# A decoder trunk on one core: some steps take two pieces of background modulation, its totals are fp32 products of the running sum, and attention's first left sides are made in the stage of v

## The chip, the cores and the metric

The kernel runs on one core of one Trainium2 chip. The metric is the device time of one execution in microseconds (us), as the median of several runs. The engines are named as the profile names them: PE (TensorE matmuls), PEld (its weight loads), DVE (VectorE), ACT (ScalarE), POOL (GpSimd) and SP (SyncE, which issues most DMAs). Every engine works through its own instructions in a fixed order and waits where an instruction's input or buffer isn't ready.

## The reference

Two layers over x of 1024 positions by 1024 features. Layer 0 mixes tokens with a gated MLP over chunks, layer 1 with attention in three dilations; a dense squared-ReLU MLP follows each. Each of the four sub-layers is modulated by a vector c:

```python
def ada_mod(c, w, b):
    m = jax.nn.silu(c) @ w + b                 # w: 1024 x 3072
    shift, scale, gate = jnp.split(m, 3, axis=-1)
    return shift[:, None, :], scale[:, None, :], 1.0 + gate[:, None, :]

for i in range(DEPTH):                          # DEPTH = 2
    shift, scale, gate = ada_mod(c, ada_w[i, 0], ada_b[i, 0])
    h = x * (1.0 + scale) + shift
    y = mixer_a(h, ...) if i % 2 == 0 else mixer_b(h, ...)
    x = layer_norm(ALPHA * x + gate * y, ln_g[i, 0], ln_b[i, 0])
    shift, scale, gate = ada_mod(c, ada_w[i, 1], ada_b[i, 1])
    h = x * (1.0 + scale) + shift
    y = jnp.square(jax.nn.relu(h @ mlp_w_up[i])) @ mlp_w_down[i]
    x = layer_norm(ALPHA * x + gate * y, ln_g[i, 1], ln_b[i, 1])
```

In `mixer_b`, h @ w_qkv gives q, k and v for three dilations and 16 heads. All of it is fp32.

## The kernel before

One program, built by a framework that orders each engine's instructions, runs the sub-layers 0 to 3 one after the other: `mixer_a`, `mlp(1)`, `attention`, `mlp(3)`. An fp32 matrix product is three matmuls of fp32r parts: a source is split into a high part (a cast on ACT, L102) and a low part (source minus high part, on DVE, L103), and the three products that matter are summed in PSUM. Large products are done in a form with seven products of half-size blocks (named 1 to 7) instead of eight, so the "left" and "right" sides of a product are blocks or sums and differences of blocks. 12 matmuls of 128x512 make one product of the up stage.

**An MLP has two stages.** In the up stage 16 chunks (`ch`) each run seven products (PE L914); their lefts, made by `make_left` five products ahead, take one ACT cast and one DVE subtraction each. DVE also adds PSUM to what was kept (`part`, L932) and forms sums of hidden rows (`s`). In the down stage (PE L1072, tiles `psd`) the hidden rows are read back as `lraw`.

**The modulation of the coming sub-layers is made in the background.** `ada_steps` turns one half (512 columns) of shift (part 0), scale (part 1) or gate (part 2) into a group of 11 small functions: eight steps that load 128x512 of `ada_w` (tile `adaw`, two buffers) and add it, times silu(c), to the running sum `adaacc` (one DVE instruction, L125 or L128), then `bias_row`, `reduce` and `total`. `reduce` splits the running sum (`adahi` on ACT, `adalo` on DVE). `total` sums over the 128 partitions on PE: for shift and scale eight matmuls of two columns (L159, L160, tile `psa`), for gate two of 512. `tick(n)` runs the next n functions of the queue; `drain()` runs all that are left. In this text a group is called by its name in the tiles, sub-layer, part and half: `3_1_0` is the first half of scale of sub-layer 3.

- `mixer_a` queues 8 groups (88 functions), calls `tick(2)` 16 times and `tick(7)` eight times, then drains.
- `mlp(1)` queues 10 groups (110 functions: six of sub-layer 2, the four of shift and scale of sub-layer 3), calls `tick()` after each of the 98 products of chunks 2 to 15, then drains: 12 functions are left for the drain.
- `mlp(3)` queues the two gate groups of sub-layer 3.

**Attention** begins with `values_stage`, which computes v for all heads (PE L1266, tiles `psv`; its weights go through the row buffers `raw` of `wts` and `res` of `work`), and evicts v by ACT and DVE copies, from where POOL stores it. Then `project()`, a generator, makes q and k of one pair of heads and one dilation after the other, again with seven products (PE L1422, tiles `psqk`). Before its first product it loads four quarters of weights (`wq`, `wk`, 128x512, in a pool that is opened after the stage of v) and makes three lefts (products 1, 2, 6). Four products are run first, then the masks are made (`near` on POOL, `far` on DVE), then the rest.

Of the kernel before, what the change touches and what calls it, by code (L numbers as in the profile page):

```python
# [10 lines left out]
F32 = mybir.dt.float32  # L11
# [24 lines left out]
def trunk(ctx: ExitStack, tc: tile.TileContext, x, c, ada_w, ada_b, ln_g, ln_b, a_w_in, a_b_in,  # L36
# [73 lines left out]
    def ada_steps(j, order):  # L110
# [4 lines left out]
        for part, h in order:  # L115
# [21 lines left out]
            def reduce(part=part, h=h, box=box):  # L137
                nm = f"{j}_{part}_{h}"
                acc = box["acc"]
                hi, lo = (ada_p.tile([P, HALF], F32R, name=f"ada{m}_{nm}", tag=f"ada{m}") for m in ("hi", "lo"))  # L140
                if part == 2:
                    V.tensor_tensor(acc[0:1, :], acc[0:1, :], box["row"][0:1, :], op=ALU.add)
                split(hi[:], lo[:], acc[:])
                box["sum"] = (hi, lo)

            def total(part=part, h=h, box=box, w0=w0):
                nm = f"{j}_{part}_{h}"
                hi, lo = box["sum"]
                pst = bank("tr", f"psa_{nm}")
                if part == 2:  # L150
                    T.matmul(pst[:], ones_r[:], hi[:], start=True, stop=False)
# [5 lines left out]
                for k in range(4):  # L157
                    w = slice(k * P, (k + 1) * P)
                    T.matmul(pst[:, 2 * k : 2 * k + 2], hi[:, w], ones_r[:, 0:2], start=True, stop=False)  # L159
                    T.matmul(pst[:, 2 * k : 2 * k + 2], lo[:, w], ones_r[:, 0:2], start=False, stop=True)  # L160
                src = pst[:, 0:8].rearrange("p (k t) -> p k t", t=2)[:, :, 0]
# [14 lines left out]
            todo.append([lambda k=k, step=step: step(k) for k in range(KD)] + [bias_row, reduce, total])  # L176
# [597 lines left out]
    def mlp(j, before):  # L774
# [21 lines left out]
        with ExitStack() as ph:  # L796


            with ExitStack() as up:
# [182 lines left out]
                for n, (ch, p) in enumerate(seq):  # L982
# [7 lines left out]
                    if ch > 1:  # L990
                        tick()
# [193 lines left out]
    def attention(before):  # L1185
# [16 lines left out]
        with ExitStack() as ph:  # L1202
            homes = {p: pool(ph, f"form{p}", 1, side="right") for p in (4, 6, 5)}

            def values_stage():
                with ExitStack() as vs:
# [83 lines left out]
                    for n, s in enumerate(steps):  # L1290
# [12 lines left out]
                        if n + SPLITS < len(steps):  # L1303
                            prepare(*steps[n + SPLITS])

# [5 lines left out]
            def perm(t, g, half=None):  # L1311

                d = DILATION[g]
                if g == 0:
                    return t if half is None else t[:, half * HALF : (half + 1) * HALF]
                if g == 1:
                    v = t.rearrange("p (r i) -> p r i", r=d)
                    n = v.shape[2] // 2
                else:
                    v = t.rearrange("p (a b i) -> p a b i", b=2, i=S // d)  # L1320
                    n = v.shape[3] // 2
                return v[..., half * n : (half + 1) * n]

            def by_pos(t, g):

                if g == 0:
                    return t
                if g == 1:
                    return t.rearrange("p (i r) -> p r i", r=4)
                return t.rearrange("p (i b a) -> p a b i", b=2, a=8)  # L1330

            order = [(hp, g) for hp in range(N_PAIRS) for g in PATTERNS]
            got = [dict() for _ in order]
            pinned = []

            def quarter(name):
                return qp.tile([P, 4, P], F32, name=name, tag="wq", bufs=4)

            PRODUCTS = (1, 2, 6, 5, 7, 3, 4)
            after = {}  # L1340

            def project():

                seq = [(n, p) for n in range(len(order)) for p in PRODUCTS]
                raw, total, left, sums, kept = {}, {}, {}, {}, {}

                def load(n, X, kh):
                    if n >= len(order):
                        return
                    hp, g = order[n]  # L1350
                    c0 = g * 3 * D + X * D + hp * P
                    t = raw[n, X, kh] = quarter(f"w{'qk'[X]}{kh}_{hp}_{g}")
                    nc.sync.dma_start(t[:], b_w_qkv[0, kh * HALF : (kh + 1) * HALF, c0 : c0 + P].rearrange("(k p) n -> p k n", p=P))

                def make_left(n, p):
                    hp, g = order[n]
                    nm = f"{hp}_{g}_{p}"
                    l11, l12, l21, l22 = (raw.get((n, X, kh)) for X in range(2) for kh in range(2))

                    def total_tile():  # L1360
                        return qp.tile([P, 4, P], F32, name=f"ws_{nm}", tag="ws", bufs=2)

                    src = {1: l11, 2: l12, 4: l22}.get(p)
                    if p == 6:
                        t5, src = total[n, 5], total[n, 6] = total_tile(), total_tile()
                        V.tensor_tensor(t5[:], l21[:], l22[:], op=ALU.add)
                        sub(src[:], t5[:], l11[:])
                    elif p == 5:
                        src = total.pop((n, 5))
                    elif p == 7:  # L1370
                        src = total_tile()
                        sub(src[:], l22[:], total[n, 6][:])
                        sub(total[n, 6][:], l12[:], total[n, 6][:])
                    elif p == 3:
                        src = total.pop((n, 6))
                    t = left[n, p] = wts.tile([P, 2, 4, P], F32R, name=f"left_{nm}", tag="whi")
                    split(t[:, 0], t[:, 1], src[:])
                    for X, kh in {6: ((0, 0),), 5: ((0, 1),), 7: ((1, 0),), 4: ((1, 1),)}.get(p, ()):
                        load(n + 1, X, kh)
                    if p == 3:  # L1380
                        for key in ((n, X, kh) for X in range(2) for kh in range(2)):
                            del raw[key]

                AHEAD = 3
                for X in range(2):
                    for kh in range(2):
                        load(0, X, kh)
                lefts = [(n, p) for n in range(len(order)) for p in (1, 2, 6, 5, 7, 4, 3)]
                for s in lefts[:AHEAD]:
                    make_left(*s)  # L1390

                def evict(n, p, acc):
                    hp, g = order[n]

                    def out(nm, half):
                        return perm(got[n][nm][:], g, half)

                    if p in (1, 6, 5):
                        t = kept[p] = work.tile([P, HALF], F32, name=f"part{p}_{hp}_{g}", tag="h")
                        A.copy(t[:], acc[:])  # L1400
                        return
                    if p == 2:
                        for nm in "qk":
                            got[n][nm] = wts.tile([P, S], F32, name=f"{nm}_{hp}_{g}", tag="wlo")
                    if p == 4:
                        A.copy(out("k", 1), by_pos(acc[:], g))
                        return
# [4 lines left out]
                for i, (n, p) in enumerate(seq):  # L1412
                    if i + AHEAD < len(seq):
                        make_left(*lefts[i + AHEAD])
# [517 lines left out]
```

## Time and profile before

| | us |
|---|---|
| median of 3 runs | 2657.34 (2653.39 to 2660.51) |
| the profiled execution's own time | 2653.4 |
| its span | 2651.7 |
| PE busy | 2588.0 (98%) |
| DVE busy | 1898.6 (72%) |
| ACT busy | 1259.1 (47%) |
| mean granted clock of PE | 0.992 |

The profiled execution stands at the fast end of the three runs, 3.9 us (0.15%) under their median. A row of the timeline gives start, duration, engine, line, operation, output<-inputs, shape and count; in brackets stands how long the engine had been idle before and what ended that. A row of the windows gives, for a stretch of the span, the busy time of each engine, then PE's granted clock, the share of the DMA engines and GB/s. Matmul durations overlap: back to back at full clock a 128x512 matmul shows 0.39 and starts 0.227 after the last.

### The profile page before, as it was taken

Reading aid. Unit: us, or ns where it says so; the run is one execution under the profiler, and the core shown is the slowest. Engines: PE = TensorE matmul, PEld = TensorE weight load, DVE = VectorE, ACT = ScalarE, POOL = GpSimd, SP = SyncE. Lnnn points to the kernel's source line nnn. Section 1 sums busy time; section 2 is a strip of 40 time slices with the busy share of each in tenths; the row PEclk is TensorE's granted clock in tenths of the full one; section 3 lists DMA queues with packets and bytes.
Section 4 is the critical chain, followed back from the end, with each engine's and each line's share of the span. In section 5 each row is a group of like instructions: output and inputs, shape, how many; then the busy total and the mean of one; then the engine's idle time right before and its main releaser. Section 6 shows DMA issues by size and latency. Waiting matters only on the chain. (4 is left out here: it accounts for less than half of the span.)

```text
span 2651.7 us, 36843 instructions
## 1 busy us (share of the span) xinstructions
PE 2588.0 (98%) x13322; PEld 2080.0 (78%) x13322; DVE 1898.6 (72%) x3462; ACT 1259.1 (47%) x2431; POOL 185.6 (7%) x213
## 2 busy tenths in 40 slices
PE   7999999999999998999999999999999999999998
PEld 6788878888788887887777777777776888878887
DVE  4677798787789677443677777767659865677987
ACT  2343285555434444322555555556517555544432
POOL 0001100000000000011212221112100000000000
PEclk8999999999999999999999999999999999999999
DMA  7354437666865643542444454544862754495562
GB/s 247 115 183 130 134 112 227 216 228 227 297 218 189 227 151 112 159 159 96 115 132 125 128 158 112 155 131 128 286 202 104 226 194 146 157 330 170 180 209 80
DMA packets 329787, 457.05 MB, mean 172 GB/s; under 512 B 51532, under 2 KB 179956, under 8 KB 329604
## 3 DMA queue, kind: packets, MB, share of 16 engines
q1 hardware_dynamic: 316548, 408.55, 48.6%
q0 software_dynamic: 13056, 46.14, 5.0%
q8 instruction: 104, 1.70, 0.3%
q14 instruction: 79, 0.65, 0.1%
HBM read 346.00 MB, written 108.61 MB: 171 GB/s over the span
## 5 line engine op out<-in xcount | busy, mean ns | idle before, releaser
L1422 PE MATMUL psqk<-right,left 128*128 128x512 f32 x2016 | 523.5, 405 | 3.4 <-DVE left L103 2.2
L1422 PEld LDWEIGHTS psqk<-right,left 128*128 128x128 f32 x2016 | 363.4, 189 | 96.2 <-issue 15.3
L914 PE MATMUL psua<-right,left 128*128 128x512 f32 x1536 | 364.5, 390 | 3.5 <-ACT right L102 1.7
L1072 PE MATMUL psd<-rhi,lhi 128*128 128x512 f32 x896 | 350.2, 391 | 2.1 <-ACT part L945 2.1
L1072 PE MATMUL psd<-rlo,lhi 128*128 128x512 f32 x896 | 349.5, 390 | 0.9 <-DVE rlo L103 0.7
L1072 PE MATMUL psd<-rhi,llo 128*128 128x512 f32 x896 | 349.4, 390 | 0.0
L914 PEld LDWEIGHTS psua<-right,left 128*128 128x128 f32 x1536 | 286.9, 188 | 66.0 <-ACT right L102 2.6
L103 DVE TENSOR_TENSOR left<-ws,left 128x512 fp32r<-128x512 f32 x224 | 164.9, 737 | 144.9 <-ACT left L102 143.2
L1489 ACT ACTIVATE p<-p,stat 128x256 f32<-128x256 f32 (+2 forms) x384 | 161.7, 422 | 154.9 <-DVE stat L1487 154.1
L1266 PE MATMUL psv<-vwhi,right 128*128 128x512 f32 x672 | 211.7, 396 | 7.2 <-ACT right L102 7.2
L1072 PEld LDWEIGHTS psd<-rhi,lhi 128*128 128x128 f32 x896 | 168.6, 188 | 37.8 <-ACT part L945 3.0
L1072 PEld LDWEIGHTS psd<-rlo,lhi 128*128 128x128 f32 x896 | 168.6, 188 | 36.3 <-DVE rlo L103 1.6
L1072 PEld LDWEIGHTS psd<-rhi,llo 128*128 128x128 f32 x896 | 168.5, 188 | 35.1
L914 PE MATMUL psuc<-right,left 128*128 128x512 f32 x768 | 188.2, 391 | 0.5 <-ACT right L102 0.4
L102 ACT CAST left<-ws 128x512 fp32r<-128x512 f32 x224 | 138.5, 619 | 95.1 <-DVE ws L835 74.8
L914 PEld LDWEIGHTS psuc<-right,left 128*128 128x128 f32 x768 | 143.4, 188 | 30.9 <-DVE right L103 0.9
L1266 PEld LDWEIGHTS psv<-vwhi,right 128*128 128x128 f32 x672 | 127.1, 190 | 35.7 <-ACT right L102 7.6
L128 DVE SCALAR_TENSOR_TENSOR adaacc<-adaw,silu_c,adaacc 128x512 f32<-128x512 f32 x140 | 107.1, 765 | 65.4 <-DMA adaw<-in_ada_w_dram 64.7
L103 DVE TENSOR_TENSOR llo<-lraw,lhi 128x1024 fp32r<-128x1024 f32 x112 | 136.3, 1217 | 0.6 <-ACT lhi L102 0.6
L1266 PE MATMUL psv<-vwlo,right 128*128 128x512 f32 x336 | 132.7, 396 | 0.2 <-DVE r L215 0.2
L1487 DVE CUSTOM_DVE_ANT_0 p<-sc,bias 128x256 f32<-128x256 f32 (+2 forms) x384 | 103.1, 323 | 40.3 <-PE sc L1575 40.1
L102 ACT CAST lhi<-lraw 128x1024 fp32r<-128x1024 f32 x112 | 117.3, 1048 | 6.7 <-PE psua L914 4.3
(264 smaller groups left out, 4407.0 us busy)
## 6 DMA issues: line engine op xcount, KB each, us to landing
lraw<-forms SPq DMA_DIRECT2D x112, 512.0 KB, 3.6
adaw<-in_ada_w_dram SPq DMA_DIRECT2D x192, 256.0 KB, 3.2
up<-in_mlp_w_up_dram SPq DMA_DIRECT2D x64, 512.0 KB, 4.9
forms<-s SPq DMA_DIRECT2D x128, 256.0 KB, 2.3
rraw<-in_mlp_w_down_dram SPq DMA_DIRECT2D x64, 512.0 KB, 4.4
forms<-part SPq DMA_DIRECT2D x96, 256.0 KB, 2.5
vraw<-in_b_w_qkv_dram SPq DMA_DIRECT2D x42, 512.0 KB, 3.9
spill<-acc SPq DMA_DIRECT2D x24, 512.0 KB, 2.6
```

The costliest lines, as they stand in the source:

```text
L102: first = A.copy(hi, src) if hi_engine is A else hi_engine.tensor_copy(hi, src)
L103: return first, lo_engine.tensor_tensor(lo, src, hi, op=ALU.subtract)
L128: ins = V.scalar_tensor_tensor(acc[:], raw[:], silu_c[:, k : k + 1], acc[:], ALU.mult, ALU.add)
L914: T.matmul(acc, w[:, a, k, :], right[p][:, b, k, :], start=p in (1, 2, 5) and k + a + b == 0, stop=k == 3 and a == 1, skip_group_check=True)
L1072: T.matmul(sums[kind, m][:], l[a][:, k, m * P : (m + 1) * P], r[b][:, k, :], start=p in (1, 5, 2, 3) and kp + k + a + b == 0, stop=kp == K ...
L1266: T.matmul(sums[own, m][:], right[p][:, b, 2 * kp + k, m * P : (m + 1) * P], w[a][:, k, :], start=new and k + a + b == 0, stop=kp + k == 2 ...
L1422: ins = T.matmul(sums[kind][:], w[:, a, k, :], right[p][:, b, k, :], start=p in (1, 2, 5) and k + a + b == 0, stop=k == 3 and a == 1, skip ...
L1487: V.tensor_tensor_reduce(out=pr, in0=src, in1=bias, scale=-0.125, scalar=3e38, op0=ALU.add, op1=ALU.min, accum_out=nm)
L1489: A.activation(pr, pr, AF.Exp, bias=nm, scale=-1.0, accum_out=l)
```

## The change

Three things are changed.

1. The groups of shift and scale have nine functions instead of 11: `bias_row` and `reduce` are gone, and `total` multiplies the running sum itself, in fp32, with a column of ones: four matmuls of one column instead of eight of two. The gate groups stay as they are.
2. In the up stage, the step after product 4 or 5 takes two functions of the queue instead of one.
3. `project()` is written ahead of `values_stage` and is started in it: its four loads are issued three steps ahead of the end of the stage of v, into row buffers (`res`, two quarters to a buffer, with the sums in the third), and the lefts of products 1 and 2 are made two steps ahead of the end; the left of product 6 when attention asks for its first product. The functions moved are otherwise unchanged.

```diff
-                if part == 2:
-                    V.tensor_tensor(acc[0:1, :], acc[0:1, :], box["row"][0:1, :], op=ALU.add)
+                V.tensor_tensor(acc[0:1, :], acc[0:1, :], box["row"][0:1, :], op=ALU.add)
                 split(hi[:], lo[:], acc[:])
                 box["sum"] = (hi, lo)
             def total(part=part, h=h, box=box, w0=w0):
...
                 for k in range(4):
                     w = slice(k * P, (k + 1) * P)
-                    T.matmul(pst[:, 2 * k : 2 * k + 2], hi[:, w], ones_r[:, 0:2], start=True, stop=False)
-                    T.matmul(pst[:, 2 * k : 2 * k + 2], lo[:, w], ones_r[:, 0:2], start=False, stop=True)
-                src = pst[:, 0:8].rearrange("p (k t) -> p k t", t=2)[:, :, 0]
+                    T.matmul(pst[:, k : k + 1], box["acc"][:, w], ones_f[:, 0:1], start=True, stop=True)
+                src = pst[:, 0:4]
...
-            todo.append([lambda k=k, step=step: step(k) for k in range(KD)] + [bias_row, reduce, total])
+            todo.append([lambda k=k, step=step: step(k) for k in range(KD)] + ([bias_row, reduce, total] if part == 2 else [total]))
...
                     next(build, None)
                     next(build, None)
                     if ch > 1:
-                        tick()
+                        tick(2 if p in (4, 5) else 1)
                 drain()
...
+            def two(name):
+                t = work.tile([P, 2, 4, P], F32, name=name, tag="res", bufs=3)
+                return [t[:, 0], t[:, 1]]
...
                 def load(n, X, kh):
...
+                    if n:
+                        t = qp.tile([P, 4, P], F32, name=f"w{'qk'[X]}{kh}_{hp}_{g}", tag="wq", bufs=4)[:]
+                    elif kh == 0:
+                        t, raw[n, X, 1] = two(f"w{'qk'[X]}_{hp}_{g}")
+                    else:
+                        t = raw[n, X, 1]
...
                 lefts = [(n, p) for n in range(len(order)) for p in (1, 2, 6, 5, 7, 4, 3)]
-                for s in lefts[:AHEAD]:
-                    make_left(*s)
+                yield
+                for s in lefts[: AHEAD - 1]:
+                    make_left(*s)
+                yield
+                make_left(*lefts[AHEAD - 1])
...
                         if n + SPLITS < len(steps):
                             prepare(*steps[n + SPLITS])
+                        if n in (len(steps) - LOADS, len(steps) - SPLITS):
+                            next(stream)
```

**Where instructions move.** First ACT at the end of the stage of v. `v4` are the last copies of v out of PSUM, `left_0_2_p` is the left of product p of the first group. Before:

```order
L102 CAST vwhi_0_4_1_9921<-vraw_0_4_1_0_9883 128x1024
L1275 COPY v4_0_0_9973<-psv1_0_0_9495 128x512
L1275 COPY v4_0_1_9976<-psv1_0_1_9499 128x512
L1275 COPY v4_0_2_9979<-psv1_0_2_9503 128x512
L1275 COPY v4_0_3_9982<-psv1_0_3_9507 128x512
L102 CAST left_0_2_1_10016<-wq0_0_2_10008 128x512
L102 CAST left_0_2_2_10019<-wq1_0_2_10010 128x512
L102 CAST left_0_2_6_10026<-ws_0_2_6_10023 128x512
```

And now:

```order
L102 CAST vwhi_0_4_1_9825<-vraw_0_4_1_0_9787 128x1024
L102 CAST left_0_2_1_9859<-wq_0_2_9829 128x512
L102 CAST left_0_2_2_9862<-wq_0_2_9829 128x512
L102 CAST left_0_2_6_9927<-ws_0_2_6_9924 128x512
L1408 COPY v4_0_0_9889<-psv1_0_0_9399 128x512
L1408 COPY v4_0_1_9892<-psv1_0_1_9403 128x512
L1408 COPY v4_0_2_9895<-psv1_0_2_9407 128x512
L102 CAST left_0_2_5_9932<-ws_0_2_6_9924 128x512
```

Three of the casts now stand ahead of the copies that wait for the last matmuls of v. DVE at the same place, before (`v6` are its evictions of v, `far` is the mask):

```order
L1279 TENSOR_TENSOR v6_0_3_9780<-psv5_0_3_9657,v6_0_3_9780 128x512
L1444 COPY far_10059<-near_10051 64x64 x2
L103 TENSOR_TENSOR left_0_2_1_10016<-wq0_0_2_10008,left_0_2_1_10016 128x512
L103 TENSOR_TENSOR left_0_2_2_10019<-wq1_0_2_10010,left_0_2_2_10019 128x512
L1366 TENSOR_TENSOR ws_0_2_6_10022<-wk0_0_2_10012,wk1_0_2_10014 128x512
L1197 TENSOR_TENSOR ws_0_2_6_10023<-ws_0_2_6_10022,wq0_0_2_10008 128x512
```

And now:

```order
L103 TENSOR_TENSOR left_0_2_1_9859<-wq_0_2_9829,left_0_2_1_9859 128x512
L1412 TENSOR_TENSOR v6_0_0_9678<-psv5_0_0_9549,v6_0_0_9678 128x512
L1412 TENSOR_TENSOR v6_0_1_9680<-psv5_0_1_9553,v6_0_1_9680 128x512
L1412 TENSOR_TENSOR v6_0_2_9682<-psv5_0_2_9557,v6_0_2_9682 128x512
L1412 TENSOR_TENSOR v6_0_3_9684<-psv5_0_3_9561,v6_0_3_9684 128x512
L103 TENSOR_TENSOR left_0_2_2_9862<-wq_0_2_9829,left_0_2_2_9862 128x512
L103 TENSOR_TENSOR left_0_2_6_9927<-ws_0_2_6_9924,left_0_2_6_9927 128x512
L103 TENSOR_TENSOR left_0_2_5_9932<-ws_0_2_6_9924,left_0_2_5_9932 128x512
L1195 TENSOR_TENSOR ws_0_2_7_9966<-wk_0_2_9832,ws_0_2_6_9924 128x512
L1195 TENSOR_TENSOR ws_0_2_6_9924<-wq_0_2_9829,ws_0_2_6_9924 128x512
L1457 COPY far_9960<-near_9952 64x64 x2
```

The low parts of the first four lefts no longer stand behind `far`.

Second, the up stage of `mlp(1)` around the total of group `3_1_0`. On PE before (`left_1_c_p` is the left of product p of chunk c):

```order
L914 MATMUL psua_1_11_4973<-right_1_4_3206,left_1_11_4_5115 128x512 x12
L914 MATMUL psuc_1_12_5200<-right_1_3_3008,left_1_12_3_5147 128x512 x12
L914 MATMUL psua_1_12_5150<-right_1_7_3205,left_1_12_7_5170 128x512 x12
L914 MATMUL psua_1_13_5320<-right_1_1_2781,left_1_13_1_5197 128x512 x12
L159 MATMUL psa_3_1_0_5335<-ones_r_78,adahi_3_1_0_5312 128x2
L160 MATMUL psa_3_1_0_5335<-ones_r_78,adalo_3_1_0_5313 128x2
```

And now, three chunks earlier:

```order
L912 MATMUL psuc_1_9_4683<-right_1_5_2974,left_1_9_5_4544 128x512 x12
L912 MATMUL psua_1_9_4633<-right_1_6_2975,left_1_9_6_4577 128x512 x12
L912 MATMUL psua_1_8_4450<-right_1_4_3174,left_1_8_4_4598 128x512 x12
L912 MATMUL psuc_1_9_4683<-right_1_3_2976,left_1_9_3_4630 128x512 x5
L158 MATMUL psa_3_1_0_4748<-ones_f_79,adaacc_3_1_0_4574 128x1 x4
L912 MATMUL psuc_1_9_4683<-right_1_3_2976,left_1_9_3_4630 128x512 x7
```

Within its chunk the total stands more than two products earlier. DVE there, before:

```order
L128 SCALAR_TENSOR_TENSOR adaacc_3_1_0_5091<-adaw_3_1_0_4_5190,silu_c_82,adaacc_3_1_0_5091 128x512
L128 SCALAR_TENSOR_TENSOR adaacc_3_1_0_5091<-adaw_3_1_0_5_5215,silu_c_82,adaacc_3_1_0_5091 128x512
L890 TENSOR_TENSOR ws_1_13_5238<-up_1_13_0_5015,up_1_13_1_5017 128x512
L128 SCALAR_TENSOR_TENSOR adaacc_3_1_0_5091<-adaw_3_1_0_6_5235,silu_c_82,adaacc_3_1_0_5091 128x512
L103 TENSOR_TENSOR left_1_13_5_5240<-ws_1_13_5238,left_1_13_5_5240 128x512
L103 TENSOR_TENSOR left_1_12_4_5284<-up_1_12_1_4846,left_1_12_4_5284 128x512
L835 TENSOR_TENSOR ws_1_13_5238<-ws_1_13_5238,up_1_13_0_5015 128x512
L835 TENSOR_TENSOR s4_1_11_5259<-part12_1_11_5255,s2_1_11_5135 128x512
L128 SCALAR_TENSOR_TENSOR adaacc_3_1_0_5091<-adaw_3_1_0_7_5262,silu_c_82,adaacc_3_1_0_5091 128x512
```

And now:

```order
L128 SCALAR_TENSOR_TENSOR adaacc_3_1_0_4574<-adaw_3_1_0_4_4673,silu_c_82,adaacc_3_1_0_4574 128x512
L128 SCALAR_TENSOR_TENSOR adaacc_3_1_0_4574<-adaw_3_1_0_5_4698,silu_c_82,adaacc_3_1_0_4574 128x512
L888 TENSOR_TENSOR ws_1_10_4724<-up_1_10_0_4493,up_1_10_1_4495 128x512
L128 SCALAR_TENSOR_TENSOR adaacc_3_1_0_4574<-adaw_3_1_0_6_4701,silu_c_82,adaacc_3_1_0_4574 128x512
L103 TENSOR_TENSOR left_1_10_5_4726<-ws_1_10_4724,left_1_10_5_4726 128x512
L103 TENSOR_TENSOR left_1_9_4_4781<-up_1_9_1_4311,left_1_9_4_4781 128x512
L128 SCALAR_TENSOR_TENSOR adaacc_3_1_0_4574<-adaw_3_1_0_7_4721,silu_c_82,adaacc_3_1_0_4574 128x512
```

The last addition of the group moved ahead of two other instructions, and the rest is alike.

Third, PE in `mixer_a` at the total of `1_1_0`, before behind the last matmul of `psu_0_1`:

```order
L328 MATMUL psu_0_1_1247<-hT_0_1_0_123,winu_0_hi_1216 128x512
L328 MATMUL psu_0_1_1247<-hT_0_1_1_124,winu_0_hi_1216 128x512
L328 MATMUL psu_0_1_1247<-hT_0_1_0_123,winu_0_lo_1217 128x512
L159 MATMUL psa_1_1_0_1273<-ones_r_78,adahi_1_1_0_1180 128x2
L160 MATMUL psa_1_1_0_1273<-ones_r_78,adalo_1_1_0_1181 128x2
```

And now behind the eleventh of its 24:

```order
L326 MATMUL psu_0_1_1254<-hT_0_1_0_123,winu_0_lo_1224 128x512
L326 MATMUL psu_0_1_1254<-hT_0_1_0_123,winu_0_hi_1223 128x512
L326 MATMUL psu_0_1_1254<-hT_0_1_1_124,winu_0_hi_1223 128x512
L158 MATMUL psa_1_1_0_1180<-ones_f_79,adaacc_1_1_0_1109 128x1 x4
L326 MATMUL psu_0_1_1254<-hT_0_1_0_123,winu_0_lo_1224 128x512
```

It moved 13 matmuls forward; DVE's rows up to the last addition of this group are the same in both. In the up stage of `mlp(1)` the last total now stands in chunk 12, and none is left for the drain.

More of the change, by code (lines that the diff above doesn't have):

```diff
@@ L1203, in attention, with perm @@
             homes = {p: pool(ph, f"form{p}", 1, side="right") for p in (4, 6, 5)}
+            qp = None
+            def perm(t, g, half=None):
+                d = DILATION[g]
+                if g == 0:
+                    return t if half is None else t[:, half * HALF : (half + 1) * HALF]
+                if g == 1:
+                    v = t.rearrange("p (r i) -> p r i", r=d)
+                    n = v.shape[2] // 2
+                else:
+                    v = t.rearrange("p (a b i) -> p a b i", b=2, i=S // d)
+                    n = v.shape[3] // 2
+                return v[..., half * n : (half + 1) * n]
@@ new lines, in by_pos @@
+            def by_pos(t, g):
+                if g == 0:
+                    return t
+                if g == 1:
+                    return t.rearrange("p (i r) -> p r i", r=4)
+                return t.rearrange("p (i b a) -> p a b i", b=2, a=8)
+            order = [(hp, g) for hp in range(N_PAIRS) for g in PATTERNS]
+            got = [dict() for _ in order]
+            pinned = []
+            def two(name):
+                t = work.tile([P, 2, 4, P], F32, name=name, tag="res", bufs=3)
+                return [t[:, 0], t[:, 1]]
@@ L1324, in by_pos @@
[L1324 to L1388, printed above, removed]
-                for s in lefts[:AHEAD]:
-                    make_left(*s)
[L1392 to L1407, printed above, removed]
-                    dst = {2: ("q", 1), 7: ("k", 0), 3: ("q", 0)}[p]
-                    t = kept.pop({2: 1, 7: 5, 3: 6}[p])
-                    V.tensor_tensor(out(*dst), by_pos(acc[:], g), by_pos(t[:], g), op=ALU.add)
-                for i, (n, p) in enumerate(seq):
-                    if i + AHEAD < len(seq):
-                        make_left(*lefts[i + AHEAD])
-                    hp, g = order[n]
-                    kind = "mb" if p in (2, 5, 3) else "mm"
-                    if p in (1, 2, 5):
-                        sums[kind] = bank(kind, f"psqk{p}_{hp}_{g}")
-                    w = left.pop((n, p))
-                    for k in range(4):
-                        for a, b in TERMS:
-                            ins = T.matmul(sums[kind][:], w[:, a, k, :], right[p][:, b, k, :], start=p in (1, 2, 5) and k + a + b == 0,
-                                           stop=k == 3 and a == 1, skip_group_check=True)
-                            if pinned:
-                                tc.keep_in_program_order(ins)
-                        if k == 3:
-                            evict(n, p, sums[kind])
-                            if (n, p) in after:
-                                after[n, p]()
-                        yield
```

95 lines of the change are left out of this document (82 added, 13 removed).

## The prediction

> **What bounds the kernel now.** I read the page first, then who waited for whom on PE, then the windows of the stages that the change touches, and last the timeline at the places where PE stood.
>
> ```profile
> span 2651.7 us, 36843 instructions
> PE 2588.0 (98%) x13322; PEld 2080.0 (78%) x13322; DVE 1898.6 (72%) x3462; ACT 1259.1 (47%) x2431; POOL 185.6 (7%) x213
> ```
>
> PE is busy 98% of the span. What the change removes from DVE and ACT is worth nothing by itself; it counts only where PE waits. PE's waits by releaser name two places:
>
> ```profile
> PE psa L159 <- ACT adahi L102: 3.6, 1, 3.6
> ...
> PE psqk L1422 <- DVE left L103: 2.2, 1, 2.2
> ...
> PE psqk L1422 <- ACT left L102: 1.2, 1, 1.2
> ```
>
> The windows show the stages around them, PE's busy time first (of 50) and DVE's third:
>
> ```profile
> 450.00:500.00 50.00, 50.00 (x230) 41.65 (x229) 37.91 (x65) 28.03 (x50) 0.00 (x0) 1.00 0.67 220
> 500.00:550.00 50.00, 50.00 (x226) 41.48 (x225) 41.21 (x69) 28.62 (x50) 0.00 (x0) 1.00 0.65 211
> 650.00:700.00 50.00, 44.73 (x195) 35.96 (x194) 36.00 (x48) 24.91 (x32) 0.00 (x0) 0.97 0.93 315
> 1200.00:1250.00 50.00, 46.65 (x195) 37.39 (x195) 18.83 (x27) 10.68 (x17) 9.70 (x18) 0.97 0.37 121
> 2150.00:2200.00 50.00, 50.00 (x222) 41.39 (x221) 29.05 (x46) 27.77 (x48) 0.00 (x0) 1.00 0.42 143
> ```
>
> In the middle of the up stage of mlp(1) PE never stands. It loses time where that stage turns into the down stage (650 to 700) and where v turns into q and k (1200 to 1250).
>
> **The end of the up stage: a gain of 5.1.** The queue of mlp(1) holds 110 functions, and 98 calls of `tick` take one each; the other 12 run in the drain, and the last total (3_0_1) falls into the down stage:
>
> ```profile
> 686.43 0.39 PE L1072 MATMUL psd<-rlo,lhi 128*128 128x512 f32 x1
> 690.40 0.27 PE L159 MATMUL psa<-ones_r,adahi 128*128 128x2 f32 x1 [3.58 <-ACT adahi L102]
> 692.34 0.77 PE L1072 MATMUL psd<-rhi,lhi 128*128 128x512 f32 x1
> ...
> 695.47 0.45 PE L1072 MATMUL psd<-rlo,lhi 128*128 128x512 f32 x1
> ```
>
> PE stands 3.58 for the cast of the running sum. After that the seven matmuls from 692.34 to 695.47 take 3.13 where seven steps of 0.227 would take 1.59: the clock has dropped, and costs 1.54. Eight groups of shift and scale lose two functions each, which leaves 94, and 28 of the 98 calls now take two, so 126 could be taken: the order puts the last total into chunk 12, and nothing is left for the drain. Gain 3.58 + 1.54 = 5.1. Shorter waits there (0.4 to 0.75 each, 1.7 together) hang on the down stage's own operands; I count them at 0, and up to 1.7 as the other end.
>
> **The end of the stage of v: a gain of 5.2.**
>
> ```profile
> 1230.07 1.29 ACT L1275 COPY v<-psv 128x512 f32<-128x512 f32 x2
> 1230.34 0.40 PE L1266 MATMUL psv<-vwlo,right 128*128 128x512 f32 x1
> 1231.26 1.14 ACT L102 CAST left<-wq 128x512 fp32r<-128x512 f32 x2
> 1231.93 0.73 PE L1422 MATMUL psqk<-right,left 128*128 128x512 f32 x2 [1.19 <-ACT left L102]
> 1233.65 0.39 DVE L1444 COPY far<-near 64x64 f32<-64x64 f32 x2 [13.43 <-POOL near L1440]
> 1234.08 1.33 DVE L103 TENSOR_TENSOR left<-wq,left 128x512 fp32r<-128x512 f32 x2
> 1234.82 6.43 PE L1422 MATMUL psqk<-right,left 128*128 128x512 f32 x20 [2.16 <-DVE left L103]
> ```
>
> The casts of the first lefts stand behind the copies of v on ACT, the low parts behind the mask `far` on DVE, which waits for POOL, which issues the stores of v. PE stands 1.19 and 2.16, and then runs 20 matmuls in 6.43: 19 steps in 6.04 instead of 4.31, 1.73 lost to the clock, and 0.1 in the pair before. In the new order both stand in front, on ACT and on DVE. What has to be there by 1230.7 is ready long before: the loads were issued as early as this,
>
> ```profile
> 1201.14 1.16 SPq L1353 DMA_DIRECT2D wq<-in_b_w_qkv_dram  x2
> ```
>
> and now wait for row buffers, of which DVE has read the last by 1210.7. SP puts two of the four ahead of the reads of v of the next group and two behind; those reads aren't wanted for 20 us, so that costs 0. DVE's evictions of v now stand behind two sums and a left; the PSUM banks that they free are wanted at 1230, 13 us later. What is late next is the left of product 6 and then 7, needed at 1230.7 + 2 x 2.72 = 1236.1 and at 1241.6; `ws` ran in 0.7 to 0.8 a piece in this place. Gain 1.19 + 2.16 + 1.73 + 0.1 = 5.2.
>
> **The totals themselves cost 1.0 more.** The two sorts of rows, with the instruction that follows each:
>
> ```profile
> 55.07 0.81 PE L595 MATMUL psa<-silu_c,adaw 128*128 128x1 f32 x6
> 55.74 0.36 PE L596 MATMUL psa<-ones_f,adaacc 128*128 128x1 f32 x2
> 666.39 0.17 PE L159 MATMUL psa<-ones_r,adahi 128*128 128x2 f32 x1
> 667.20 0.48 PE L1072 MATMUL psd<-rhi,lhi 128*128 128x512 f32 x1
> ```
>
> An fp32 matmul of one column leaves two records: line 595 is written for three matmuls there and shows six in 0.67, 0.112 each. A total of four is 8 x 0.112 = 0.89; the old one of eight was 667.20 - 666.39 = 0.81. Twelve groups: 12 x 0.08 = 1.0, on PE and so on the path. [...]
>
> The removed casts and subtractions (12 each) lie beside PE and are worth 0; so does `bias_row`.
>
> **Waits that the new totals bring: 4.5.** The total now stands right behind the last addition, with no split between, and the order moves it forward on PE; behind it stand all later products. In mixer_a:
>
> ```profile
> 155.61 0.75 DVE L128 SCALAR_TENSOR_TENSOR adaacc<-adaw,silu_c,adaacc 128x512 f32<-128x512 f32 x1 [0.49 <-DMA adaw<-in_ada_w_dram]
> 158.71 0.17 PE L159 MATMUL psa<-ones_r,adahi 128*128 128x2 f32 x1
> 171.62 0.75 DVE L128 SCALAR_TENSOR_TENSOR adaacc<-adaw,silu_c,adaacc 128x512 f32<-128x512 f32 x1 [0.81 <-DMA adaw<-in_ada_w_dram]
> ```
>
> The total of 1_1_0 moves 13 matmuls forward, to 158.71 - 13 x 0.227 = 155.8, and DVE's addition ends at 156.4: PE waits 0.6. For 1_0_0 the addition ends at 172.4 and PE arrives at about 171.3 (behind the first of the small matmuls that start at 170.6, and 0.6 late): 1.0. The next two come out at 0 and 0.4, walked in the same way with a pair of loads every 3.0 to 3.7. Sum 2.0; the ends are 0.5 and, with 3.7 for every pair, 6.5.
>
> In the up stage of mlp(1), DVE around the last additions of 3_1_0:
>
> ```profile
> 591.08 0.68 DVE L932 TENSOR_TENSOR part<-psub,part 128x512 f32<-128x512 f32 x1
> 593.03 0.75 DVE L128 SCALAR_TENSOR_TENSOR adaacc<-adaw,silu_c,adaacc 128x512 f32<-128x512 f32 x1
> 595.78 0.75 DVE L128 SCALAR_TENSOR_TENSOR adaacc<-adaw,silu_c,adaacc 128x512 f32<-128x512 f32 x1 [1.99 <-DMA adaw<-in_ada_w_dram]
> 598.44 0.68 DVE L103 TENSOR_TENSOR left<-up,left 128x512 fp32r<-128x512 f32 x1
> 600.65 0.75 DVE L128 SCALAR_TENSOR_TENSOR adaacc<-adaw,silu_c,adaacc 128x512 f32<-128x512 f32 x1
> ```
>
> and PE beside it:
>
> ```profile
> 598.55 2.88 PE L914 MATMUL psuc<-right,left 128*128 128x512 f32 x12
> ```
>
> The last addition moves ahead of two instructions, to 599.0, and ends at 599.8. The new total stands behind five matmuls of the product that starts at 598.55, at 599.7. So PE waits about 0.1 in an instance where a load was 2 us late, and the three totals in this place wait 0 to 1. For 2_1_1 and 2_0_1, counted from the eviction of product 7, additions and lefts reach the total in 6.9 to 8.0 where PE needs 7.0 to 7.3: 0 to 1 each. The two gate groups keep their split and have over 1 us to spare. I take 2.5 for the stage; the ends are 0 and 12 (ten totals at 1.2 each).
>
> **DVE's load there.** The window without background (29.05) and the two with it (39.6 on average) price it at 10.5 in 50 us, or 18.4 functions. Now 23.6 functions come in 50 us, 2.6 groups, each 7 x 0.67 + 0.41 + 0.3 = 5.4 when they are of shift and scale: 14.1, so DVE goes to 43. Its waits in one window before:
>
> ```profile
> DVE adaacc L128 <- DMA adaw<-in_ada_w_dram: 5.0, 3, 2.4
> DVE left L103 <- ACT left L102: 3.9, 3, 2.8
> ```
>
> 43 + 5.0 leaves 2 of 50. DVE keeps up, but barely.
>
> **The sum.** -5.1 - 5.2 + 1.0 + 2.0 + 2.5 = -4.8 against the execution's own 2653.4: 2648.6. It stands 3.9 under the median, so the forecast beside the median of 2657.34 is 2652.5, 0.18% faster; its own range is 2647 to 2657.
>
> **Rivals.**
> - The totals find their sums ready everywhere. For it speaks that no total but one waited before, against it the two waits worked out in mixer_a. -5.1 - 5.2 + 1.0 = -9.3, with the short waits -11.0: 2646 to 2648.
> - DVE becomes the bound in the up stage of mlp(1). In each of nine chunks it has about 0.8 to spare (2 of 50, times 19.5). If the pairs of `adaw` take the 4.6 of the row at 595.78 throughout (591.1 to 595.8) instead of 3.5, three of the four pairs of a chunk cost up to 1.1 more each: 3.3 - 0.8 = 2.5 a chunk, 22 in nine chunks, less the 11 us or so by which lefts are ahead; 11 to 22 lost, net +4 to +15: 2661 to 2672. It decides from a pair time of about 3.8. For it speaks the DMA share of 0.65 to 0.67, which the denser loads raise; against it that most additions in those windows waited for nothing.
> [...]
> - The first lefts don't come early, because a load or a row buffer is late: the 5.2 stays lost, 2657.7.
>
> **How the numbers follow.** Forecast 0.45, no waits 0.32, DVE bound 0.14, four passes 0.02, late lefts 0.07. A measurement tells no more than about 0.3% (8 us) from no change. Faster by more than that: most of the second case and a sixth of the first, 0.35. Slower: most of the third, 0.12. Within: 0.53. The range takes in 2646 less 3 of run-to-run spread, and reaches into the third case: 2643 to 2666.
>
> **What the profile after would show.** No `psa` behind 667 and no granted clock under 1 at 692; `psqk` following `psv` within 0.3 and clock 1.00 there; eight records of about 0.11 in a total; `psa` on line 158 with waits for DVE `adaacc`, 0 to 1 us each, first in mixer_a. The forecast is wrong if those waits sum to over 10, if PE starts to wait for `left` between 430 and 600, or if a new gap stands in front of the first `psd` or `psqk`.

## The result: 0.85% slower, and where the profile shows it

The changed kernel takes 2679.9 us (median of four, 2677.24 to 2682.1) beside 2656.4 for the kernel before: ratio 1.0085, 95% interval 1.0068 to 1.0101. The profiled execution took 2677.24, its span 2675.5. The forecast was 2652.5 in a range of 2643 to 2666.

The head of the page after:

```profile
span 2675.5 us, 36815 instructions
PE 2597.1 (97%) x13322; PEld 2080.3 (78%) x13322; DVE 1891.9 (71%) x3450; ACT 1251.2 (47%) x2419; POOL 182.7 (7%) x213
```

DVE and ACT do less, PE as many matmuls in more time. PE's waits after, by releaser, in the lines that bear on the argument:

```profile
PE psa L158 <- DVE adaacc L128: 11.9, 9, 2.2
PE pT L1603 <- ACT p L1502: 6.3, 4, 2.0
...
PE psa L150 <- ACT adahi L102: 3.2, 3, 1.2
PE psd L1070 <- ACT part L943: 3.0, 2, 1.5
...
PE psa L151 <- DVE adalo L103: 1.6, 1, 1.6
```

The waits of `psqk` for its lefts (1.2 and 2.2) and the 3.6 of the last total are gone. In their place nine totals wait for their running sums, 11.9 in all, and the gate totals, whose code is untouched, wait 4.8 (0.9 before). The windows that were shown of before, now. The third and fourth are moved by 24.7 and 20.2, so that they hold the same work: the first `psd` stands at 691.89 instead of 667.20, the last `psv` at 1250.55 instead of 1230.34.

```profile
450.00:500.00 50.00, 47.16 (x209) 38.67 (x210) 37.83 (x66) 23.37 (x41) 0.00 (x0) 0.97 0.68 217
500.00:550.00 50.00, 48.92 (x214) 39.74 (x213) 42.86 (x70) 26.90 (x47) 0.00 (x0) 1.00 0.73 235
...
674.70:724.70 50.00, 48.38 (x205) 39.24 (x204) 32.71 (x34) 25.79 (x32) 0.00 (x0) 0.97 0.93 328
1220.20:1270.20 50.00, 50.00 (x220) 40.87 (x219) 21.91 (x31) 12.07 (x19) 8.96 (x18) 1.00 0.35 116
...
2150.00:2200.00 50.00, 50.00 (x222) 41.42 (x221) 29.26 (x47) 27.45 (x48) 0.00 (x0) 1.00 0.51 173
```

At the two places that the prediction wanted to mend PE is busier: 48.38 instead of 44.73 at the turn to the down stage, where a granted clock of 0.97 remains, and 50.00 instead of 46.65 where v turns into q and k. The middle of the up stage, where PE never stood, now loses 1 to 3 us of every 50 in the windows shown, and one of them shows a granted clock of 0.97.

To see each stage by itself, take the start of the first instruction of a tile that begins a stage (`psu` mixer_a, `psua` the up stage of mlp(1), `psd` its down stage, `psv` the stage of v, `pT` the first transposes of attention, `psd_wo` its end) and subtract:

| from, to | before | after | difference |
|---|---|---|---|
| start to mixer_a | 147.8 | 142.5 | -5.3 |
| mixer_a (`psu` to `psd_wout`) | 108.5 | 121.3 | +12.7 |
| up stage of mlp(1) | 320.0 | 337.3 | +17.3 |
| first `psd` to first `psv` | 317.1 | 312.5 | -4.6 |
| first `psv` to first `pT` | 284.4 | 279.1 | -5.4 |
| first `pT` to first `psd_wo` | 636.3 | 646.5 | +10.2 |
| the rest | 837.5 | 836.4 | -1.1 |

The gains came (-4.6 and -5.4), and two stages lost three times as much (+30). The start and attention run the same instructions in the same order in both kernels; the experiments below show that these two rows differ from one execution to the next.

**One wait, step by step.** PE around the total of 3_0_0, `x8` being the eight records of its four fp32 matmuls:

```profile
601.73 1.75 PE L912 MATMUL psuc<-right,left 128*128 128x512 f32 x7
604.79 1.02 PE L158 MATMUL psa<-ones_f,adaacc 128*128 128x1 f32 x8 [1.31 <-DVE adaacc L128]
605.67 1.51 PE L912 MATMUL psuc<-right,left 128*128 128x512 f32 x5
606.99 4.20 PE L912 MATMUL psua<-right,left 128*128 128x512 f32 x11
```

and DVE's additions of that sum ahead of it:

```profile
597.38 0.75 DVE L128 SCALAR_TENSOR_TENSOR adaacc<-adaw,silu_c,adaacc 128x512 f32<-128x512 f32 x1 [1.25 <-DMA adaw<-in_ada_w_dram]
600.38 0.75 DVE L128 SCALAR_TENSOR_TENSOR adaacc<-adaw,silu_c,adaacc 128x512 f32<-128x512 f32 x1 [2.24 <-DMA adaw<-in_ada_w_dram]
...
603.89 0.75 DVE L128 SCALAR_TENSOR_TENSOR adaacc<-adaw,silu_c,adaacc 128x512 f32<-128x512 f32 x1 [0.18 <-DMA adaw<-in_ada_w_dram]
```

Three of the last four additions waited for their load, the last ended at 604.6, and the total stood in the middle of a product since 603.5. Then comes a second price: 11 matmuls from 606.99 take 4.20, the first seven steps at 0.43 each instead of 0.227. Windows of 3.4 us, laid on the start of that slow stretch, show it (PE's busy time first, its granted clock in the third column from the end):

```profile
600.00:603.40 3.40, 3.40 (x16) 2.55 (x14) 3.00 (x5) 1.63 (x3) 0.00 (x0) 1.00 0.39 128
...
603.40:606.80 3.40, 2.09 (x14) 1.86 (x14) 2.61 (x6) 0.79 (x3) 0.00 (x0) 1.00 0.61 157
606.80:610.20 3.40, 3.40 (x10) 2.62 (x9) 2.24 (x6) 2.34 (x4) 0.00 (x0) 0.50 0.97 355
610.20:613.60 3.40, 3.40 (x16) 2.77 (x16) 2.15 (x4) 1.89 (x3) 0.00 (x0) 1.00 0.07 27
```

A window with 1.31 of wait and 1.0 of one-column matmuls is followed by exactly one window at half clock, which costs 3.41 x 0.5 = 1.7. By the granted clock in windows of 2 us, mixer_a loses 5.1 in this way (three such windows) and the up stage 5.1; before lost nothing in either. So mixer_a's 12.7 is 6.7 of waits and 5.1 of clock, with some 0.9 left over, and the up stage's 17.3 is 9.5 of waits of the totals and 5.1 of clock, with 2.7 left over. Most of what is left over can be accounted for. The idle time before a total is counted from where a matmul's record of 0.39 ends, though the next could have started 0.227 after its start, so each wait costs some 0.16 more than it shows: 0.8 for five waits in mixer_a, 1.3 for eight in the up stage. And the total 3_0_1 itself (0.9) now stands in the up stage's row; before it stood in the next one.

### The profile page after: what moved, and what is told of

Its sections match the earlier page's. It is cut to its first block, busy times and chain, and to the rows that moved or that the text cites. A ratio compares the mean times of both kernels' runs of the same rounds, so it can differ in the third digit from the quotient of the medians.

```text
span 2675.5 us, 36815 instructions
## 1 busy us (share of the span) xinstructions
PE 2597.1 (97%) x13322; PEld 2080.3 (78%) x13322; DVE 1891.9 (71%) x3450; ACT 1251.2 (47%) x2419; POOL 182.7 (7%) x213
```

## Experiments

Each kernel was timed in five rounds beside the kernel before on the same chip. The stages in us, by the same starts as above:

| kernel | median | ratio (95%) | mixer_a | up stage | `psd` to `psv` | `psv` to `pT` |
|---|---|---|---|---|---|---|
| lead | 2662.8 | 1.0022 (1.0009 to 1.0035) | 114.6 | 331.7 | 312.5 | 279.1 |
| density | 2669.9 | 1.0052 (1.0035 to 1.0069) | 115.0 | 340.2 | 310.9 | 279.0 |
| one_a_call | 2663.7 | 1.0026 (1.0015 to 1.0037) | 123.8 | 324.5 | 312.5 | 279.1 |
| project_only | 2651.7 | 0.9977 (0.9965 to 0.9988) | 108.7 | 319.3 | 320.0 | 278.0 |
| split_two | 2658.0 | 1.0014 (1.0000 to 1.0027) | 108.3 | 332.5 | 311.0 | 278.5 |
| split_one | 2651.0 | 0.9987 (0.9974 to 1.0000) | 108.2 | 330.2 | 310.0 | 278.6 |
| four_buffers | 2643.5 | 0.9954 (0.9937 to 0.9970) | 107.0 | 321.2 | 310.9 | 279.2 |
| lead_four | 2643.6 | 0.9960 (0.9947 to 0.9972) | 107.8 | 320.3 | 313.0 | 278.9 |
| before_four | 2652.3 | 0.9985 (0.9977 to 0.9994) | 107.8 | 319.3 | 316.5 | 284.2 |
| split_two_four | 2646.5 | 0.9961 (0.9948 to 0.9974) | 107.8 | 322.3 | 312.5 | 278.9 |
| one_four | 2646.5 | 0.9961 (0.9948 to 0.9974) | 107.0 | 320.8 | 310.9 | 279.3 |
| three_buffers | 2644.4 | 0.9960 (0.9946 to 0.9974) | 107.0 | 321.9 | 312.5 | 278.8 |

**First set: where the total stands, the pace of the additions, and the moved `project()`.**

The run `lead`, against the changed kernel:

```diff
-([bias_row, reduce, total] if part == 2 else [total])
+([bias_row, reduce, total] if part == 2 else [lambda: None, lambda: None, total])
```

> The changed kernel with two empty functions put back ahead of each total of shift and scale: a group is 11 functions long again, so the total stands three calls behind the last addition, as before. All else of the change stays (fp32 totals, two functions in positions 4 and 5, project ahead). Theory A, lead: PE waits because the total stands right behind the last addition. Then the waits of psa for adaacc go (11.9 us in the changed kernel, to under 2), and with them the clock drops of 1.7 us each that follow them (three in mixer_a, three in the up stage): 2679.9 - 12 - 10 = about 2658, less what the rest of the change gains, 2650 to 2660. Theory B, density: PE waits because the additions come faster than the pairs of loads of adaw and DVE can follow. Mixer_a is as before (its 12 us come back), the up stage still takes two functions in two positions and keeps most of its loss: 2665 to 2672, with psa waits between 430 and 630 left.

Measured 2662.8, between the two ranges: 17 of 23 us came back, but not the mechanism that A states. Five totals still wait for their sums, one of them for 2.7:

```profile
PE psa L158 <- DVE adaacc L128: 8.0, 5, 2.7
PE psa L150 <- ACT adahi L102: 2.7, 2, 1.6
```

Mixer_a, where the pace is that of before, kept 6 of its 12.7. Neither theory foresaw that. The order on PE shows a part of the reason: the total that waits 2.27 in mixer_a stands behind 98 matmuls of that stage, as in the changed kernel (129 before). The empty functions put it later in the queue, but not on PE.

The run `density`:

```diff
-([bias_row, reduce, total] if part == 2 else [total])
+([bias_row, reduce, total] if part == 2 else [total, lambda: None, lambda: None])
```

> The changed kernel with the two empty functions behind each total of shift and scale instead of ahead: the pace of additions is that of the run with lead, but the total still stands right behind the last addition. Theory A, lead: the waits stay, 8 to 12 us of psa for adaacc and several clock drops: 2672 to 2682. Theory B, density: mixer_a is as before, up stage partly: 2660 to 2670.

2669.9, just inside B's range, but by chance: B wanted mixer_a as before and a part of the up stage's loss back, and neither came so. Mixer_a is at 115.0 as with `lead`: there it made no difference on which side of the total the empty functions stood, the slower pace gave back half. The up stage was at its worst (340.2): its totals wait as much as in the changed kernel (9.6 in nine waits), and five windows at half clock stand in it instead of three. On PE `lead` has the totals of the up stage at most 14 matmuls later than `density`, some 3 us, so the two runs part the theories only weakly.

The run `one_a_call`:

```diff
-                        tick(2 if p in (4, 5) else 1)
+                        tick()
```

> The changed kernel with one function a call in the up stage of mlp(1), as before, instead of two in positions 4 and 5. 94 functions still fit in 98 calls. Theory A, lead: the totals in the up stage still stand right behind their last additions, about as many waits: 2674 to 2682. Theory B, density: the up stage loses its waits (about 13 us with its clock drops), mixer_a keeps its 12: 2663 to 2669.

2663.7 and an up stage of 324.5: B, the pace. 12.8 of the stage's 17.3 us came with the second function in positions 4 and 5; mixer_a kept its loss (123.8).

The run `project_only`, against the changed kernel (the whole of `ada_steps` is that of before again):

```diff
-                    T.matmul(pst[:, k : k + 1], box["acc"][:, w], ones_f[:, 0:1], start=True, stop=True)
+                    T.matmul(pst[:, 2 * k : 2 * k + 2], hi[:, w], ones_r[:, 0:2], start=True, stop=False)
+                    T.matmul(pst[:, 2 * k : 2 * k + 2], lo[:, w], ones_r[:, 0:2], start=False, stop=True)
...
-                        tick(2 if p in (4, 5) else 1)
+                        tick()
```

> The kernel before with the move of project() alone: its first loads in row buffers, first lefts made in the stage of v. In the two profiles the way from v to the first transposes of attention is 5.4 us shorter, and attention from there to its end is 10.2 longer with the same order of instructions on PE, DVE and ACT. Theory C, the 10 us of attention differ from run to run and have nothing to do with the move: 2651 (5 less than before, 0.998). Theory D, they come with it (another phase of the lefts or of the loads): 2661 (1.002).

2651.7, theory C: a gain of 5.6 where 5.2 was forecast. Its attention took 636.9 from the first `pT` to the first `psd_wo`, and in the eleven other runs of this study it took 637 to 641; the 646.5 of the changed kernel's profile was not seen again. The start of the program ranged from 141.9 to 148.4 over all profiles. So the +10.2 and -5.3 of the table above probably don't belong to the change. That isn't shown for the changed kernel itself, whose other three executions have no trace: without these two rows its stages make +18.9, while the medians differ by 23.5. Against `project_only`, attention in the changed kernel's profile has 5.5 more of waits (14.3 instead of 8.7) and one window at half clock; what brought them is not settled.

**Second set: what makes the sums late.** In the first set both the place of the total and the pace mattered, and DVE's additions kept waiting for loads. So either the split had been the cover of the total, or the loads are the cause.

The run `split_two` is the changed kernel with the `ada_steps` of before, `split_one` the same with fewer double calls. Against `project_only`:

```diff
-                        tick()
+                        tick(2 if p in (4, 5) else 1)
```

```diff
-                        tick()
+                        tick(2 if p == 4 else 1)
```

> The changed kernel with the totals of before (bias_row, reduce with the split, eight fp32r matmuls), keeping two functions in positions 4 and 5 and project ahead. Seen so far: the turn from up to down is 4.6 us shorter with an empty queue there (317.1 to 312.5 us from the first psd to the first psv), project alone gives 2651.7. Theory A2, the split between last addition and total is the cover of the total: mixer_a as before (108.6), the up stage of mlp(1) within 2 us of before (320 to 322), 2651.7 - 4.6 = 2647 to 2649. Theory B2, the pace of two functions in positions 4 and 5 by itself costs in the up stage (one function a call gave back 13 of its 17 us): 326 to 333 there, 2653 to 2660.

> As split_two, with two functions in position 4 alone: 14 more calls than before, 112 for 110 functions, so that nothing is left for the drain, at a pace only a seventh over that of before. Theories A2 and B2 both: mixer_a as before, up stage 320 to 323, the turn 4.6 shorter: 2647 to 2650, which would be the best of the kernels here. If the last total falls so close to the end of the up stage that it waits again: 2651 to 2655.

2658.0 is B2: with the split back, mixer_a is as before (108.3), but the up stage takes 332.5, and the totals wait for the split instead of the sum:

```profile
PE psa L159 <- ACT adahi L102: 4.8, 5, 1.4
PE psa L151 <- ACT adahi L102: 1.7, 1, 1.7
```

`split_one` was a miss: 2651.0, and in the profile (an execution of 2655.4) an up stage of 330.2 where 320 to 323 was expected. Only a seventh more calls brought four waits (5.0 us) and two windows at half clock. So the up stage of before stood close to the edge, and the second part of the change pushed it over by itself.

The run `four_buffers`, against the changed kernel, in the two places where a tile `adaw` is made:

```diff
-tag="adaw", bufs=2)
+tag="adaw", bufs=4)
```

> The changed kernel with four buffers for adaw instead of two. Theory E, the sums are late because a load of adaw is only issued when the addition two before has freed its buffer: DVE's waits for adaw in the up stage (22 us between 400 and 660) fall under 8, PE's waits of psa for adaacc from 11.9 to under 4, clock drops with them: 2654 to 2662. Theory F, the order counts on the loads and moves the totals forward as far as the buffers allow, or DVE's other work makes the sums late: 2672 to 2684.

2643.5, better than theory E's range: 36 us under the changed kernel and 11.5 under before. DVE's waits for loads between 400 and 660, in the kernel before:

```profile
DVE adaacc L128 <- DMA adaw<-in_ada_w_dram: 18.9, 13, 2.9
```

in the changed kernel with two buffers:

```profile
DVE adaacc L128 <- DMA adaw<-in_ada_w_dram: 22.3, 25, 2.2
...
DVE adaacc L125 <- DMA adaw<-in_ada_w_dram: 5.8, 3, 2.9
```

with four:

```profile
DVE adaacc L128 <- DMA adaw<-in_ada_w_dram: 3.1, 5, 1.4
```

DVE waited for loads in the kernel before too, but no total of these two stages waited for its sum there. The totals didn't move back on PE for the four buffers: but for one that stands three matmuls later, they stand where they did in the changed kernel or earlier, by up to 12 matmuls in the up stage and by more in mixer_a. All but one, which waits 0.3, find their sums ready. And DVE has more to do than in any window shown so far, while PE doesn't stand:

```profile
500.00:550.00 50.00, 50.00 (x226) 41.48 (x225) 44.30 (x74) 28.92 (x48) 0.00 (x0) 1.00 0.73 245
```

That rules out DVE as the bound. With two buffers a load is issued when the addition two before it has read its buffer, and lands 2.8 to 4.5 us later (median 3.3, from the profile of before); a pair of loads takes about that long at least, and SP, which issues them, stood 41.2 us between 400 and 660 behind earlier loads of `adaw` (13.7 before, 1.0 with four buffers):

```profile
SPq L122 <- DMA adaw<-in_ada_w_dram: 41.2, 27, 3.8
```

The run `lead_four` is `lead` with the same edit.

> The run with lead (two empty functions ahead of each total, 2662.8) with four buffers for adaw instead of two. Theory E: the waits that were left there (2.3 and 1.6 in mixer_a, 2.7, 1.3, 1.1 and 1.7 in the up stage) go, and with them three clock drops: mixer_a 109.5, up stage 321 to 323, 2649 to 2653. Theory F: nothing moves, 2658 to 2666.

2643.6, theory E, again under its range, with no wait of `psa` left in either stage. The place of the total is worth nothing once the loads are in time.

**Third set: what four buffers do alone, and what each part of the change is worth with them.**

`before_four` is the kernel before with the edit of `four_buffers`, `split_two_four` is `split_two` with it, `one_four` is `one_a_call` with it. `three_buffers`, against the changed kernel:

```diff
-tag="adaw", bufs=2)
+tag="adaw", bufs=3)
```

> The kernel before with four buffers for adaw instead of two, nothing else. Theory G, the buffers help only where totals wait for their sums: before had no such wait in mixer_a and the up stage but the one of 3.6 us at the turn, which comes from the drain and stays: 2653 to 2657, the same as before within 2 us. Theory H, four buffers are worth 10 us by themselves and the change nothing: 2643 to 2647.

2652.3, a little under G's range: 3.9 under before, not 10. The last total still waits in the turn, 2.4 instead of 3.6. Against this kernel the change with four buffers gains 8.8 by the medians (8.2 by the two ratios, each taken beside the kernel before on its own chip).

> Project ahead, two functions in positions 4 and 5, the totals of before (split, eight matmuls) and four buffers for adaw: the run with four buffers less the new totals. If the new totals are worth nothing by themselves: 2642 to 2645, as the run with four buffers (2643.5). If the split costs DVE and ACT time that the up stage needs at this pace: up stage 324 to 330 instead of 321, 2646 to 2652.

> The run with four buffers with one function a call in the up stage instead of two in positions 4 and 5. Pace no longer matters when the loads are issued four ahead: 2642 to 2646. If the two functions in a call do gain something beyond the empty drain: 2647 or more.

2646.5 both, between the two cases that were expected or at the edge of the second. The up stage of `split_two_four` takes 322.3, not 324 to 330, with 1.7 of it for one window at half clock that stands behind no total. Neither the new totals nor the two functions a call can be told from nothing once the loads are in time: the intervals of the two ratios hold that of `four_buffers`. `one_four` empties the queue ahead of the turn through the new totals alone (94 functions in 98 calls), `split_two_four` through the double calls alone; either is enough.

> The changed kernel with three buffers for adaw instead of two (four gave 2643.5, two 2679.9). With two buffers a pair of additions took 3.0 to 4.6 us, 1.5 to 2.3 a load; two functions in positions 4 and 5 make four additions follow each other in some 6 us there. If one more load in flight is enough: 2643 to 2648. If the bursts need the fourth: psa waits of 2 to 6 us and one or two clock drops of 1.7 stay, 2650 to 2660.

2644.4: one more load in flight is enough. DVE still waits 12.5 us between 400 and 660, but PE only 1.1 in all, in three pieces, and with no clock drop in mixer_a or the up stage.

The best versions are the changed kernel with three or four buffers, 0.9960 and 0.9954 of before, not told apart.

## Why the prediction was wrong, point by point

- **The end of the up stage, -5.1: right for the wait, near in size in part by luck.** The last total is gone from the turn, and its wait of 3.58 with it. The 1.54 of clock didn't come in this profile: a window at half clock still stands there (from 695.56), now behind a wait of 1.51 for `part`, where waits of 0.75 and 0.57 stood before that the prediction counted at 0. The row is 4.6 shorter all the same (317.1 to 312.5): waits are 3.4 of it, and 0.8 is the total itself, which only moved into the row of the up stage. In profiles without that slow window the row is 310.9: a gain of 6.2, or 5.4 without the moved total.
- **The end of the stage of v, -5.2: right.** The row is 5.4 shorter, and the whole time of `project_only` 5.6. The first `psqk` follows the last `psv` without a gap, and its 23 matmuls run at full clock:

```profile
1250.55 0.40 PE L1399 MATMUL psv<-vwlo,right 128*128 128x512 f32 x1
1250.78 5.38 PE L1326 MATMUL psqk<-right,left 128*128 128x512 f32 x23
```

- **The totals themselves, +1.0: right.** Eight records, and the product behind starts 605.67 - 604.79 = 0.88 later, as against 0.81 before. The chances give 0.02 to totals of four passes: no run here shows such passes. What the trace shows is two records a matmul and the 0.88.
- **"Waits that the new totals bring: 4.5": the step that failed.** It was 2.0 for mixer_a and 2.5 for the up stage; the stages lost 12.7 and 17.3. Two things were wrong in it. The waits were mis-sized: 6.7 and 9.5 measured. In mixer_a the first two totals came out as walked (0.6 and 1.3 for 0.6 and 1.0), the next two, taken at 0 and 0.4, waited 2.05 and 0, and a gate total that wasn't in the sum waited 2.8. The reckoning took the loads at a pair every 3.0 to 3.7 and looked at single instances of a timeline in which the pace had been slower; at the new pace the loads, two in flight, were late for most totals: in the up stage eight of ten waited. The two gate groups of that stage "have over 1 us to spare", the text said; one of them waited 0.97. And a term was missing altogether: the clock. In both gaps before, the prediction had priced the slow stretch behind a wait (1.54 and 1.73), but of the new waits it counted the bare idle time. Six windows of 1.7 came with them, 10.2 us. The text's own sign of being wrong, waits for `adaacc` of over 10 in all, came true with 11.9.
- **The range.** The ends that the text itself gave for the waits were 6.5 and 12. Together they give -9.3 + 18.5 = +9, 2666 with the shift to the median, which is also where the stated range ended; with the clock's 10 it would have come within 4 us of the result.
- **The rivals.** "DVE becomes the bound" pointed at the right place, the loads of `adaw` at the pace of two functions, and gave 2661 to 2672, the nearest to what came. But its mechanism, DVE with no time left, is refuted: `four_buffers` has more DVE work in the window from 500 to 550 (44.30 instead of 42.86) and no wait of PE there. The rival that the sums are ready everywhere gave -9.3; three or four buffers make it true, and against `before_four` the change then gains 8.8.

## What to carry to other kernels

Before work in the background is packed closer, count its loads in flight against the time from issue to landing: here two buffers of 256 KB, landing in 3.3 us, held back a chain that needed four additions in two products, and a third buffer was worth some 35 us, more than the change itself in either sign. PE paid here for late operands twice, once for the wait (1.31 at the total of 3_0_0) and, where the wait fell so, once for the clock behind it (1.7); a wait of 1 to 2 us belongs into a sum at its own length and, as its other end, with the slow stretch that the same profile shows behind its neighbours. And when an operation is taken out between a producer and a consumer, what it did as cover can be part of its price, even where its own time was hidden: with two buffers mixer_a took 108.3 with the split, 114.6 with empty functions in its place and 121.3 without either.

## What the runs showed of the hardware

In the profiles looked at, the half clock comes in stretches that start on a fixed grid of 3.41 us. In the changed kernel's profile the seven slow stretches looked at start at 169.91, 204.04, 449.80, 582.92, 606.81, 695.56 and 1432.84; six of them last 3.41, the one from 204.04 twice that. The first and the last start 1262.93 apart, which is 370 x 3.4133, and modulo 3.4133 the starts are 2.65 to 2.67, every one; in `one_a_call` four starts all give 1.00. Whether a wait cost 1.7 more went with how it fell on the grid, with one exception. The cleanest case is the wait of 1.51 for `part` at the start of the down stage of mlp(1), which the waits of ten profiles show with 1.5. In `one_four` it stands from 668.32 to 669.83, across the boundary at 669.66; the clock stays at 1.00, and the row from `psd` to `psv` is 310.9, as it is in `density` and `four_buffers`. In the changed kernel it lies within a window (693.12 to 694.63, in 692.15 to 695.56), and so it does in `one_a_call` (684.53 to 686.04, in 683.67 to 687.08), `split_two_four` (669.32 to 670.83, in 668.07 to 671.49) and `three_buffers` (668.82 to 670.33, in 667.25 to 670.67); a slow one follows, and the row is 312.5, as it is in `lead` (`lead_four` 313.0). In `split_two` it lies within a window too, beginning 0.4 after its start, and none follows: the row is 311.0. The longest wait in the up stage, 2.15 at 491.26, lies across a boundary too, PE is busy for half or more of each of the two windows (1.71 and 2.94 of 3.40), and the clock stays:

```profile
487.40:490.80 3.40, 1.71 (x8) 1.09 (x6) 2.39 (x5) 1.14 (x2) 0.00 (x0) 1.00 0.91 305
490.80:494.20 3.40, 2.94 (x17) 2.62 (x18) 2.37 (x6) 1.85 (x3) 0.00 (x0) 1.00 0.93 324
```

PE's busy share alone doesn't decide it. In the window around the 1.51 of the changed kernel PE is busy for as much as in the first of these two (1.79), and a slow one follows it:

```profile
692.15:695.56 3.41, 1.79 (x7) 1.09 (x7) 3.41 (x5) 3.06 (x5) 0.00 (x0) 1.00 1.01 374
```

The 2.05 at 203.92 in mixer_a lies within one window, and two slow ones follow:

```profile
200.60:204.00 3.40, 1.35 (x7) 0.81 (x5) 3.40 (x6) 0.00 (x0) 0.00 (x0) 1.00 0.51 154
204.00:207.40 3.40, 3.40 (x12) 3.03 (x13) 2.13 (x5) 0.00 (x0) 0.00 (x0) 0.51 0.29 86
207.40:210.80 3.40, 3.40 (x9) 2.64 (x8) 1.53 (x3) 0.00 (x0) 0.00 (x0) 0.50 0.82 251
```

The wait of 1.31 together with a total of one-column matmuls was enough for a slow window (606.81 to 610.22), and so was the 1.51 without one (695.56 to 698.97). What decides beyond the place on the grid stays open. Why the second slow window follows in mixer_a, with PE busy throughout the first, was not tested; the total itself, at half clock and 1.78 long, lies at the boundary.
